# The highest cosine column of a Fourier stage: four partial products in four 32-column strips of TensorE, summed by one more product

## The chip, the cores and the metric

The kernel runs on one core of a Trainium2 chip. Five engines run their own instruction lists in order: PE (TensorE, matrix products into PSUM), DVE (VectorE), ACT (ScalarE), POOL (GpSimd) and SP (SyncE), which here issues most DMAs. An engine waits for another by semaphores. The metric is the device time of one execution in microseconds; a time "before" is the median of three runs.

## The reference

A layer of a diffusion transformer on 2048 positions by 1024 channels: a projection into thirteen pieces, then three branches (short convolution, Fourier mixing, neighbourhood attention), gates, an output projection and a final norm. The change lies in the Fourier branch:

```
def fourier_mix(u):
    b, l, w = u.shape
    ug = u.reshape(b, l, N_FGROUPS, w // N_FGROUPS).astype(jnp.float32)
    y = jnp.fft.fft2(ug, axes=(1, 3), norm='ortho').real
    return y.reshape(b, l, w).astype(u.dtype)
```

Four groups of 128 channels are transformed along 2048 positions and along the 128 channels, and the real part is kept. Only 65 of 128 cosine columns along the channels differ. Columns 0 to 63 of all groups are handled in blocks; column 64 (the highest cosine) of the four groups makes four rows of 2048, and this small product is what the change touches.

## The kernel before

The big projection is made of "pairs": each computes two 128-row output tiles for two blocks by seven products `B11, B21, T2, T1, T3, B22, T4` of 12 matmuls each (lines 315 to 317, 128x512, operands split into a high and a low part; tile `mm`, three PSUM banks). DVE, ACT and POOL prepare the weights (`wh` on ACT, line 131; `wl` on DVE or POOL, line 132) and empty the results (lines 346 to 358 and 428 on DVE).

In the second half of the program a generator, `both()`, yields small steps of attention, then of `fourier()`, between these pair steps. What the generator issues is ordered against the pair's work by a scheduler that writes one fixed list per engine; each engine then keeps to its list.

`fourier()` does for each group g of four:

- SP loads the input `fu` (1 MB, line 1023) into a buffer that it shares with `fold` of the group before, so that the load waits for the last product that reads that `fold`;
- DVE makes even and odd parts `ueo` (lines 1027 and 1030) and folds them to four tiles `fold` (lines 1034 to 1037), POOL fixes single columns (1028, 1031, 1038);
- PE multiplies each fold by the channel table (`s`, line 1044, c = 0 to 3, one PSUM bank for all), and DVE copies the result out to `X` and column 64 to `X64` (1045, 1047) before the next product may write the bank; one more product gives the middle row, copied to `xrow` and `xrow64` (1050 to 1052).

Then the transform along positions. For column 64 (line 1061 on) two halves `par` each take four products of `X64` (128 positions x 4 groups, a stationary operand of 4 columns) with a table tile `tab` of 128x512 (256 KB, six buffers, line 1057), added up in one bank (line 1065), plus the product of the middle row for `par` 0 (1067), and DVE writes the rows out to `y64` (1074, 1075). The blocks of columns 0 to 63 follow with products at lines 1086 and 1094, which take 32 more table tiles; their results `Ym` and `Yr` are stored by SP (1112, 1114). At line 541, early in the program, `mod()` already uses the form that the change brings: products with 32 stationary columns that write four strips of 32 partitions of one bank.

Of the kernel before, what the change touches and what calls it, by code (L numbers as in the profile page):

```python
# [11 lines left out]
F32 = mybir.dt.float32  # L12
F32R = mybir.dt.float32r
AF = mybir.ActivationFunctionType
ALU = mybir.AluOpType
AX = mybir.AxisListType
# [43 lines left out]
def emit(tc, I, out, dbg=None):  # L60
    nc = tc.nc
    dbg = dbg or {}
    stop = dbg.get("stop", "")
    es = ExitStack()

    def pool(stack, name, bufs=1, space=None, side=None):
        kw = {} if space is None else {"space": space}
        if space is not DRAM:
            kw["reuse_waits"] = "tile"
        if side:  # L70
            return Aligned(stack, lambda n_, b_: tc.tile_pool(name=n_, bufs=b_, side=side, **kw), name, bufs)
        return stack.enter_context(tc.tile_pool(name=name, bufs=bufs, **kw))
# [6 lines left out]
    def ctile(name, shape, dt=F32):  # L79
        return cp.tile(shape, dt, tag=name, name=name)  # L80
# [7 lines left out]
    ident = ctile("ident", [128, 128])  # L88
# [58 lines left out]
    def stage():  # L147
        return st.tile([128, 512], F32, tag="st", name="st")
# [856 lines left out]
    def fourier():  # L1005
        ef = ExitStack()
        fp = pool(ef, "fp", 1, None, "right")
        pf = pool(ef, "pf", 1, PSUM)
        X = [fp.tile([128, 4, 4, 64], F32, tag=f"X{c}", name=f"X{c}") for c in range(4)]
        X64 = fp.tile([128, 2, 4, 4], F32, tag="X64", name="X64")  # L1010
        xrow = fp.tile([1, 4, 64], F32, tag="xrow", name="xrow")
        xrow64 = fp.tile([1, 4], F32, tag="xrow64", name="xrow64")
        dct = fp.tile([128, 66], F32, tag="dct", name="dct")
        dst = fp.tile([128, 64], F32, tag="dst", name="dst")
        altr = fp.tile([1, 512], F32, tag="altr", name="altr")
        altc = fp.tile([128, 2], F32, tag="altc", name="altc")
        one2 = fp.tile([1, 2], F32, tag="one2", name="one2")
# [3 lines left out]
        for g in range(4):  # L1021
# [18 lines left out]
            for c in range(4):  # L1040
                w_ = 66 if c < 2 else 64
                ps = pf.tile([128, 4, 128], F32, tag="s1", name="s1")
# [3 lines left out]
                if c < 2:  # L1046
                    nc.vector.tensor_copy(X64[:, c, :, g], ps[:, :, 64])
                yield
            ps = pf.tile([128, 4, 128], F32, tag="s1", name="s1")
# [5 lines left out]
        def table(c, lt):  # L1055
            t = fp.tile([128, 512], F32, tag="tab", name="tab", bufs=6)
            nc.sync.dma_start(t, I["dft"][c, lt])
            return t
# [1 line left out]

        y64 = fp.tile([4, S], F32, tag="big0", name="y64")
        for par in range(2):
            ps = pf.tile([4, 512], F32, tag="x1", name="x1", bufs=2)
            for lt in range(4):
                nc.tensor.matmul(ps, X64[:, par, lt, :], table(par, lt), start=lt == 0, stop=par == 1 and lt == 3)
            if par == 0:
                nc.tensor.matmul(ps, xrow64, altr, start=False, stop=True)
                pe = pf.tile([128, 2], F32, tag="x2", name="x2", bufs=2)
                for lt in range(4):
                    nc.tensor.matmul(pe[:4], X64[:, 0, lt, :], altc, start=lt == 0, stop=False)  # L1070
                nc.tensor.matmul(pe[:4], xrow64, one2, start=False, stop=True)
                nc.vector.tensor_copy(y64[:, 1024:1025], pe[:4, 0:1])
            lo = 1 if par == 0 else 0
            nc.vector.tensor_copy(y64[:, par:1024:2], ps)
            nc.vector.tensor_copy(y64[:, 2048 - par - 2 * lo : 1024 : -2], ps[:, lo:])
            yield
        for g in range(4):
            store(fd[2 + g // 2][(g % 2) * 64 : (g % 2) * 64 + 1, :], y64[g : g + 1, :])
        for t in range(2):
            Ym = fp.tile([128, S], F32, tag="big0", name="Ym")  # L1080
            Yr = fp.tile([128, S], F32, tag="big1", name="Yr")
            for par in range(2):
                gs = slice(2 * t, 2 * t + 2)
                x1 = pf.tile([128, 512], F32, tag="x1", name="x1", bufs=2)
                for lt in range(4):
                    nc.tensor.matmul(x1, X[par][:, lt, gs, :].rearrange("p a b -> p (a b)"), table(par, lt), start=lt == 0,  # L1086
                                     stop=par == 1 and lt == 3)
# [16 lines left out]
                if par == 0:  # L1104
                    pe = pf.tile([128, 2], F32, tag="s1", name="pe")
# [33 lines left out]
    def both():  # L1139
        yield from attention()  # L1140
        vcs.close()
        yield from fourier()
        yield from tail_pools()
# [88 lines left out]
    def branch_bank():  # L1232
        return pc.tile([128, 512], F32, tag="pb", name="pb", bufs=3) if next(turn_) % 2 else bank()

    for b in range(NB):
# [5 lines left out]
        for j in range(8):  # L1241
            acc = None
            for n_, br in enumerate("afc"):
# [3 lines left out]
                ps = branch_bank()  # L1247
# [15 lines left out]
        for t in range(4):  # L1263
# [5 lines left out]
            for x in range(2):  # L1269
# [3 lines left out]
                ps = pc.tile([128, 512], F32, tag="po", name="po")  # L1273
# [106 lines left out]
```

## Time and profile before

| | |
|---|---|
| median of three runs | 2183.29 us (2179.79 to 2183.55) |
| the profiled execution's own time | 2184.33 us |
| its span, first to last instruction | 2182.5 us |
| PE busy | 2111.9 us, 97% of the span |
| DVE, ACT, POOL busy | 64%, 46%, 42% |
| DMA | 336.76 MB, 154 GB/s on average |
| mean granted TensorE clock | 0.987 of full speed |

The profile's times count from the span's start. A row of a timeline gives start, duration, engine, line, operation, output and inputs, shapes and a count; in brackets stands how long the engine had been idle before and what ended that. Matmuls overlap by their pipeline, so the distance between starts, and not the duration, says what one costs. One f32 product is two PE instructions. The Fourier stage lies at about 1520 to 1660 us.

### The profile page before, as it was taken

The page shows a single profiled execution, that of the slowest core. Times are in us where ns is not written, and L with a number is a line of the kernel's source. Part 1 is how long each engine was busy: PE and PEld are TensorE (multiplying, and loading weights), DVE is VectorE, ACT ScalarE, POOL GpSimd, SP SyncE. Part 2 cuts the span into 40 slices and gives each one's busy share as a digit, 9 for nine tenths or more (in the row PEclk, how much of TensorE's full clock was granted, in tenths as well). Part 3 has the DMA queues.
Part 4 walks back from the last instruction along what each step waited for, and adds up shares of the span by engine and source line. Part 5 has one row for each costly group of instructions (what it writes and reads, how often), then busy time and mean ns, then how long its engine had stood idle before and what let it go on. Part 6 is the DMA issues. An engine that isn't in the chain of part 4 may idle for free. (4 is left out here: it accounts for less than half of the span.)

```text
span 2182.5 us, 31772 instructions
## 1 busy us (share of the span) xinstructions
PE 2111.9 (97%) x10612; PEld 1677.0 (77%) x10612; DVE 1394.5 (64%) x2438; ACT 1006.1 (46%) x2191; POOL 907.3 (42%) x701
## 2 busy tenths in 40 slices
PE   7899999999999899999999999999999999999998
PEld 4678888888878687877777777777756778888887
DVE  5774477785765764566677776764735686575752
ACT  3643322334544533466676677776213443233321
POOL 0153477755454654444444344332413241414140
PEclk9899999999999999999999999999999999999999
DMA  8234542346333244344443544543466676666661
GB/s 294 64 120 132 168 145 82 133 168 224 104 102 104 91 142 138 103 129 124 136 145 119 157 144 136 160 148 114 163 206 213 204 242 226 209 221 203 200 196 68
DMA packets 199438, 336.76 MB, mean 154 GB/s; under 512 B 22314, under 2 KB 89194, under 8 KB 198123
## 3 DMA queue, kind: packets, MB, share of 16 engines
q1 hardware_dynamic: 185306, 309.30, 44.5%
q10 hardware_dynamic: 13968, 25.43, 3.1%
q8 instruction: 84, 1.38, 0.3%
q14 instruction: 80, 0.65, 0.1%
HBM read 248.27 MB, written 86.38 MB: 153 GB/s over the span
## 5 line engine op out<-in xcount | busy, mean ns | idle before, releaser
L131 ACT CAST wh<-wr 128x512 fp32r<-128x512 f32 x372 | 229.9, 620 | 458.6 <-PE mm L316 372.1
L132 DVE TENSOR_TENSOR wl<-wr,wh 128x512 fp32r<-128x512 f32 x248 | 238.8, 965 | 43.0 <-ACT wh L131 42.4
L132 POOL TENSOR_TENSOR wl<-wr,wh 128x512 fp32r<-128x512 f32 x124 | 168.0, 1359 | 193.8 <-ACT wh L131 180.0
L342 POOL TENSOR_TENSOR ws<-wr 128x512 f32<-128x512 f32 x62 | 82.3, 1327 | 329.5 <-DMA wr<-w_in 304.2
L373 DVE SCALAR_TENSOR_TENSOR st<-mm,bin,tp 128x512 f32<-128x512 f32 x152 | 113.7, 748 | 141.4 <-PE mm L317 131.9
L132 POOL TENSOR_TENSOR wbl<-wr,wbh 128x512 fp32r<-128x512 f32 x96 | 125.0, 1303 | 159.7 <-ACT wbh L131 151.8
L132 POOL TENSOR_TENSOR wl<-ws,wh 128x512 fp32r<-128x512 f32 x62 | 86.0, 1386 | 124.9 <-ACT wh L131 107.3
L131 ACT CAST wbh<-wr 128x512 fp32r<-128x512 f32 x96 | 59.6, 621 | 146.0 <-DMA wr<-w_br 94.0
L938 PE MATMUL tr<-ident,P 128*128 128x128 f32 (+3 forms) x672 | 119.1, 278 | 4.3 <-ACT PT L948 2.4
L428 DVE TENSOR_TENSOR st<-mm,tp 128x512 f32<-128x512 f32 x96 | 65.9, 686 | 88.5 <-PE mm L317 77.5
L360 POOL TENSOR_TENSOR wr<-wr 128x512 f32<-128x512 f32 x62 | 84.9, 1369 | 83.8 <-DVE wl L132 68.1
L344 POOL TENSOR_TENSOR wr<-ws,wr 128x512 f32<-128x512 f32 x62 | 86.0, 1387 | 77.0 <-DVE wl L132 37.9
L904 ACT ACTIVATE P<-P,sm 128x736 f32<-128x736 f32 (+5 forms) x128 | 104.7, 818 | 25.8 <-DVE sm L903 25.1
L938 PEld LDWEIGHTS tr<-ident,P 128*128 128x128 f32 (+3 forms) x672 | 80.3, 138 | 44.2 <-DVE PT L948 15.7
L317 PE MATMUL mm<-B11h,wl 128*128 128x512 f32 x248 | 99.9, 403 | 9.1 <-DVE wl L132 9.1
L317 PE MATMUL mm<-B22h,wl 128*128 128x512 f32 x260 | 104.1, 400 | 1.9 <-POOL wl L132 1.9
L315 PE MATMUL mm<-B22h,wh 128*128 128x512 f32 x260 | 104.7, 403 | 1.2 <-ACT wh L131 1.2
L316 PE MATMUL mm<-B22l,wh 128*128 128x512 f32 x260 | 103.5, 398 | 0.0
L132 POOL TENSOR_TENSOR KL<-rawk,KH 128x384 fp32r<-128x384 f32 (+1 forms) x64 | 81.4, 1280 | 46.8 <-ACT KH L131 45.3
L315 PE MATMUL mm<-B11h,wh 128*128 128x512 f32 x248 | 100.7, 406 | 0.0
L126 PE MATMUL po<-wo,mh 128*128 128x512 f32 x256 | 99.7, 390 | 0.3 <-DVE u L1170 0.3
L316 PE MATMUL mm<-B11l,wh 128*128 128x512 f32 x248 | 99.9, 403 | 0.0
(370 smaller groups left out, 6343.7 us busy)
## 6 DMA issues: line engine op xcount, KB each, us to landing
wr<-w_in SPq DMA_DIRECT2D x132, 512.0 KB
gd<-st ACTq DMA_DIRECT2D x96, 256.0 KB
wr<-w_br SPq DMA_DIRECT2D x96, 256.0 KB
tg<-gd SPq DMA_DIRECT2D x96, 256.0 KB
tab<-dft SPq DMA_DIRECT2D x40, 256.0 KB
wa<-w_ada SPq DMA_DIRECT2D x32, 256.0 KB
rawq<-qd SPq DMA_DIRECT2D x64, 128.0 KB
rawk<-kd SPq DMA_DIRECT2D x64, 128.0 KB
```

Of the source, the lines that this page charges most:

```text
L126: nc.tensor.matmul(ps, ah, bh, start=first, stop=False)
L131: heng.copy(hi, src) if heng is nc.scalar else heng.tensor_copy(hi, src)
L132: return leng.tensor_tensor(lo, src, hi.bitcast(F32), ALU.subtract)
L315: nc.tensor.matmul(ps, w[0][:, s], oh, start=first and k == 0, stop=False)
L316: nc.tensor.matmul(ps, w[0][:, s], ol, start=False, stop=False)
L317: nc.tensor.matmul(ps, w[1][:, s], oh, start=False, stop=last and k == 3)
L342: ptt(t1, a21, a22, ALU.add)
L344: ptt(a11, t1, a11, ALU.subtract)
L360: ptt(a12, a12, a11, ALU.subtract)
L373: state["ev"] = stt(dst, ps, bc(m), add, ALU.add, ALU.add)
L904: nc.scalar.activation(P[:, : CT + n], P[:, : CT + n], AF.Copy, scale=sm[:, 6:7])
L938: nc.tensor.transpose(pt[:w_, x * 128 : x * 128 + 128], src, ident)
```

## The change

`X64` and `xrow64` get 32 columns per part, of which 28 are zeros set by POOL. The four products of a half write four strips of 32 partitions of one bank instead of adding up in one place. ACT copies that bank to SBUF (`parts`), and one product with a 0/1 matrix `sel4` (made by DVE from the identity) adds the four strips into four rows. One `yield` is added per half.

```
-        X64 = fp.tile([128, 2, 4, 4], F32, tag="X64", name="X64")
+        X64 = fp.tile([128, 2, 4, 32], F32, tag="X64", name="X64")
+        nc.gpsimd.memset(X64, 0.0)
+        sel4 = fp.tile([128, 4], F32, tag="sel4", name="sel4")
+        nc.vector.tensor_reduce(sel4, ident.rearrange("p (c v) -> p v c", v=32)[:, 0:4, :], AX.X, ALU.add)
...
+        xrow64 = fp.tile([1, 32], F32, tag="xrow64", name="xrow64")
+        nc.gpsimd.memset(xrow64, 0.0)
...
-            ps = pf.tile([4, 512], F32, tag="x1", name="x1", bufs=2)
+            four = pf.tile([128, 512], F32, tag="x1", name="x1", bufs=2)
             for lt in range(4):
-                nc.tensor.matmul(ps, X64[:, par, lt, :], table(par, lt), start=lt == 0, stop=par == 1 and lt == 3)
+                nc.tensor.matmul(four[lt * 32 : lt * 32 + 32], X64[:, par, lt, :], table(par, lt), start=True, stop=par == 1 or lt > 0)
             if par == 0:
-                nc.tensor.matmul(ps, xrow64, altr, start=False, stop=True)
+                nc.tensor.matmul(four[0:32], xrow64, altr, start=False, stop=True)
+            parts = stage()
+            nc.scalar.copy(parts, four)
+            yield
+            ps = pf.tile([4, 512], F32, tag="x1", name="x1s", bufs=2)
+            nc.tensor.matmul(ps, sel4, parts, start=True, stop=True)
```

The scheduler writes other lists for the engines. Up to group 1 of the Fourier stage they agree but for the three new small instructions; from group 2 on they differ for some 270 rows of PE's list, and then agree again. Lines of the changed kernel are 4 to 10 higher (1044 is now 1048, 1065 is 1069, 1086 is 1096).

On PE, from the last product of group 2 (`s<-dst,fold`) on, the list before has the rest of the pair's `B21`, and then `T2`, `T1`, `T3` and the start of `B22` ahead of group 3's first product (`s<-dct,fold`); its first rows are:

```order
L1044 MATMUL s_16068<-dst,fold 128x64 x4
L317 MATMUL mm<-B21h_6199,wl_16320 128x512
L315 MATMUL mm<-T2h_6226,wh_16365 128x512
L316 MATMUL mm<-T2l_6227,wh_16365 128x512
L1050 MATMUL s_16074<-dct,ueo 1x66
L317 MATMUL mm<-T2h_6226,wl_16366 128x512
L315 MATMUL mm<-T2h_6231,wh_16365 128x512
L316 MATMUL mm<-T2l_6232,wh_16365 128x512
L317 MATMUL mm<-T2h_6231,wl_16366 128x512
```

In the changed kernel the same place on PE reads, down to the first two products of group 3:

```order
L1048 MATMUL s_16072<-dst,fold 128x64 x4
L315 MATMUL mm<-B21h_6195,wh_16325 128x512
L316 MATMUL mm<-B21l_6196,wh_16325 128x512
L317 MATMUL mm<-B21h_6195,wl_16326 128x512
L1054 MATMUL s_16078<-dct,ueo 1x66
L315 MATMUL mm<-B21h_6199,wh_16325 128x512
L316 MATMUL mm<-B21l_6200,wh_16325 128x512
L317 MATMUL mm<-B21h_6199,wl_16326 128x512
L1048 MATMUL s_16117<-dct,fold 128x66 x4
L1048 MATMUL s_16143<-dct,fold 128x66 x4
```

Group 3's first product stands behind 6 pair matmuls instead of 38 (counted from group 2's last product), and the second directly behind the first, where 8 pair matmuls stood between them. The pair's `T2`, `T1`, `T3` and `B22` now come behind the column-64 products.

On PE, the products of column 64 (`x<-tab,X` and what stands between them) before:

```order
L1044 MATMUL s_16139<-dct,fold 128x66 x4
L1065 MATMUL x_16185<-tab,X_15742 4x512 x2
L1044 MATMUL s_16146<-dst,fold 128x64 x4
L1065 MATMUL x_16185<-tab,X_15742 4x512
L1044 MATMUL s_16152<-dst,fold 128x64 x4
L1065 MATMUL x_16185<-tab,X_15742 4x512
L1050 MATMUL s_16180<-dct,ueo 1x66
L1070 MATMUL x_16199<-altc,X_15742 4x2 x4
L1065 MATMUL x_16230<-tab,X_15742 4x512
L1067 MATMUL x_16185<-altr,xrow_15744 4x512
L1071 MATMUL x_16199<-one_15749,xrow_15744 4x2
L1065 MATMUL x_16230<-tab,X_15742 4x512 x3
```

And on PE in the changed kernel (`x1s` is the sum of the four strips, `st` the copy that ACT makes):

```order
L1069 MATMUL x_16189<-tab,X_15742 32x512
L1048 MATMUL s_16150<-dst,fold 128x64 x4
L1069 MATMUL x_16189<-tab,X_15742 32x512 x3
L1080 MATMUL x_16229<-altc,X_15742 4x2 x4
L1048 MATMUL s_16156<-dst,fold 128x64 x4
L1054 MATMUL s_16184<-dct,ueo 1x66
L1071 MATMUL x_16189<-altr,xrow_15747 32x512
L1081 MATMUL x_16229<-one_15753,xrow_15747 4x2
L1117 MATMUL pe<-altc,X_15738 128x2 x4
L1118 MATMUL pe<-one_15753,xrow 128x2
L1076 MATMUL x1s<-st,sel_15744 4x512
L1069 MATMUL x_16238<-tab,X_15742 32x512 x4
```

The first strip product is apart from its three fellows, the four of the second half stand together, and small products that were later (`pe`) stand between the last addend and the sum.

On DVE, group 3's work before, from the copies of the middle row of group 2 on:

```order
L1052 COPY xrow_15744<-s_16074 1x1
L346 TENSOR_TENSOR tp<-mm,tp 128x512
L132 TENSOR_TENSOR wl_16490<-wr_16292,wh_16489 128x512
L1027 TENSOR_TENSOR ueo<-fu 128x1023
L1030 TENSOR_TENSOR ueo<-fu 128x1023
L350 TENSOR_TENSOR tp<-mm,tp 128x512
L1034 TENSOR_TENSOR fold<-ueo 128x512
L1035 TENSOR_TENSOR fold<-ueo 128x512
L1036 TENSOR_TENSOR fold<-ueo 128x512
L1037 TENSOR_TENSOR fold<-ueo 128x511
L1045 COPY X_15738<-s_16113 128x4x64
```

And on DVE after the change:

```order
L1056 COPY xrow_15747<-s_16078 1x1
L1031 TENSOR_TENSOR ueo<-fu 128x1023
L1034 TENSOR_TENSOR ueo<-fu 128x1023
L1038 TENSOR_TENSOR fold<-ueo 128x512
L1039 TENSOR_TENSOR fold<-ueo 128x512
L1040 TENSOR_TENSOR fold<-ueo 128x512
L1041 TENSOR_TENSOR fold<-ueo 128x511
L1049 COPY X_15738<-s_16117 128x4x64
```

The three instructions for the pair (`tp`, `wl`, `tp`) that stood among group 3's are gone from there.

## Rows read from the trace of the kernel before

**Rows 1.** The page, busy time of each engine.

```profile
PE 2111.9 (97%) x10612; PEld 1677.0 (77%) x10612; DVE 1394.5 (64%) x2438; ACT 1006.1 (46%) x2191; POOL 907.3 (42%) x701
```

**Rows 2.** PE's timeline, 1573 to 1602 us: products of groups 2 and 3.

```profile
1575.90 1.03 PE L1044 MATMUL s<-dst,fold 128*128 128x64 f32 x8
1576.75 0.47 PE L317 MATMUL mm<-B21h,wl 128*128 128x512 f32 x1
...
1586.69 1.08 PE L1044 MATMUL s<-dct,fold 128*128 128x66 f32 x8 [0.63 <-DVE fold L1034]
...
1589.98 1.08 PE L1044 MATMUL s<-dct,fold 128*128 128x66 f32 x8 [0.31 <-DVE X L1047]
```

**Rows 3.** Chain that ended last, 1539 to 1590 us: start, length, what.

```profile
1541.41 4.74 DMA fu<-fud
...
1576.97 5.17 DMA fu<-fud
```

**Rows 4.** DVE's timeline, 1573 to 1590 us.

```profile
1582.23 1.23 DVE L1027 TENSOR_TENSOR ueo<-fu 128x1023 f32<-128x1023 f32 x1 [0.51 <-DMA fu<-fud]
...
1584.51 0.68 DVE L350 TENSOR_TENSOR tp<-mm,tp 128x512 f32<-128x512 f32 x1
1585.11 1.44 DVE L1034 TENSOR_TENSOR fold<-ueo 128x512 f32<-128x512 f32 x1
...
1589.35 0.41 DVE L1045 COPY X<-s 128x256 f32<-128x256 f32 x1
```

**Rows 5.** POOL's timeline, 1573 to 1592 us.

```profile
1587.62 0.09 POOL L1031 MEMSET ueo<- 128x2 f32 x1
```

**Rows 6.** PE's timeline, 1589 to 1602 us: products of column 64.

```profile
1597.94 1.02 PE L1067 MATMUL x<-altr,xrow 1*4 1x512 f32 x2
...
1598.92 2.74 PE L1065 MATMUL x<-tab,X 128*4 128x512 f32 x6
1601.59 0.70 PE L1086 MATMUL x<-tab,X 128*128 128x512 f32 x1
```

**Rows 7.** PE's timeline, 41 to 44 us: the strips of `mod()`.

```profile
41.91 1.07 PE L541 MATMUL pr<-wa,sf 128*32 128x256 f32 x16
42.91 0.50 PE L608 MATMUL mm<-B11h,w1h 128*128 128x512 f32 x1
```

**Rows 8.** ACT, DVE and PE in the timeline, 1589 to 1625 us: copies, small products.

```profile
1596.99 0.21 DVE L1051 COPY xrow<-s 1x64 f32<-1x64 f32 x1 [0.64 <-PE s L1050]
...
1608.95 0.95 PE L1107 MATMUL pe<-altc,X 128*128 128x2 f32 x8
...
1622.88 0.59 ACT L1097 COPY st<-x 128x512 f32<-128x512 f32 x1 [5.66 <-PE x L1094]
```

**Rows 9.** POOL's groups by form: a memset of 128x256.

```profile
L521 POOL MEMSET sf<- 128x256 f32 x1 | 0.3, 311 | 0.0
```

**Rows 10.** PE's timeline, 1636 to 1647 us: a wait and what follows.

```profile
1637.55 0.39 PE L317 MATMUL mm<-T2h,wl 128*128 128x512 f32 x1
1637.77 0.39 PE L315 MATMUL mm<-T2h,wh 128*128 128x512 f32 x1
1640.42 2.69 PE L1086 MATMUL x<-tab,X 128*128 128x512 f32 x4 [2.25 <-DMA tab<-dft]
...
1643.33 0.63 PE L317 MATMUL mm<-T2h,wl 128*128 128x512 f32 x1
1643.76 0.63 PE L315 MATMUL mm<-T2h,wh 128*128 128x512 f32 x1
```

**Rows 11.** Stages: length, each engine's busy time (instructions), granted clock, DMA.

```profile
1640.00:1680.00 40.00, 37.79 (x144) 27.88 (x145) 20.37 (x44) 10.26 (x16) 13.05 (x11) 0.91 0.65 216
```

**Rows 12.** PE's waits, 1560 to 1725 us: total, times, longest.

```profile
PE po L1135 <- DVE dg L1133: 1.8, 1, 1.8
```

**Rows 13.** Chain that ended last, 1560 to 1700 us.

```profile
1627.76 12.62 DMA tab<-dft
...
1659.82 9.43 DMA fd<-Yr
```

More of the change, by code (lines that the diff above doesn't have):

```diff
@@ L1009, in fourier @@
         X = [fp.tile([128, 4, 4, 64], F32, tag=f"X{c}", name=f"X{c}") for c in range(4)]
-        X64 = fp.tile([128, 2, 4, 4], F32, tag="X64", name="X64")
+        X64 = fp.tile([128, 2, 4, 32], F32, tag="X64", name="X64")
+        nc.gpsimd.memset(X64, 0.0)
+        sel4 = fp.tile([128, 4], F32, tag="sel4", name="sel4")
+        nc.vector.tensor_reduce(sel4, ident.rearrange("p (c v) -> p v c", v=32)[:, 0:4, :], AX.X, ALU.add)
         xrow = fp.tile([1, 4, 64], F32, tag="xrow", name="xrow")
-        xrow64 = fp.tile([1, 4], F32, tag="xrow64", name="xrow64")
+        xrow64 = fp.tile([1, 32], F32, tag="xrow64", name="xrow64")
+        nc.gpsimd.memset(xrow64, 0.0)
         dct = fp.tile([128, 66], F32, tag="dct", name="dct")
@@ L1062, in fourier @@
         for par in range(2):
-            ps = pf.tile([4, 512], F32, tag="x1", name="x1", bufs=2)
+            four = pf.tile([128, 512], F32, tag="x1", name="x1", bufs=2)
             for lt in range(4):
-                nc.tensor.matmul(ps, X64[:, par, lt, :], table(par, lt), start=lt == 0, stop=par == 1 and lt == 3)
+                nc.tensor.matmul(four[lt * 32 : lt * 32 + 32], X64[:, par, lt, :], table(par, lt), start=True, stop=par == 1 or lt > 0)
             if par == 0:
-                nc.tensor.matmul(ps, xrow64, altr, start=False, stop=True)
+                nc.tensor.matmul(four[0:32], xrow64, altr, start=False, stop=True)
[4 more added lines that the diff above has]
+            nc.tensor.matmul(ps, sel4, parts, start=True, stop=True)
+            if par == 0:
                 pe = pf.tile([128, 2], F32, tag="x2", name="x2", bufs=2)
                 for lt in range(4):
-                    nc.tensor.matmul(pe[:4], X64[:, 0, lt, :], altc, start=lt == 0, stop=False)
-                nc.tensor.matmul(pe[:4], xrow64, one2, start=False, stop=True)
+                    nc.tensor.matmul(pe[:4], X64[:, 0, lt, :4], altc, start=lt == 0, stop=False)
+                nc.tensor.matmul(pe[:4], xrow64[:, :4], one2, start=False, stop=True)
                 nc.vector.tensor_copy(y64[:, 1024:1025], pe[:4, 0:1])
```

## The prediction

> **What bounds the kernel now.** I read the page first. The reader is to see there that PE is busy for 97% of the span [rows 1], so that an edit counts by what it does to PE's list: the work on it, and the idle time that opens or closes between its entries. Then I read PE's own timeline around the Fourier stage, with PE's waits beside it: between 1560 and 1725 us only four waits carry a name, 2.25 us for a table [rows 10], 1.8 us for DVE's `dg` [rows 12], and under 0.7 us each for a fold or a copy of `X` [rows 2]. Third comes the chain that ended last. It runs here through the load of `fu`, DVE's folds and the `s` products, and not through the pair matmuls [rows 3, 4]. So two strands run side by side: the Fourier chain, which waits most of its time on a DMA and on DVE, and the pair matmuls, which fill PE meanwhile. As long as there is enough filling between two steps of the chain, the chain costs only its own PE work.
>
> The order of the changed kernel shows that this filling is moved. That, and not the saved products, is where I expect most of the effect.
>
> **The change part by part.** All in us of the profiled execution.
>
> *A, the products.* Six PE instructions of the old form take from 1598.92 to 1601.59, 2.67 us [rows 6], so one product (two instructions) costs 0.89, and the eight that go cost 7.1. The new form is shown by `mod()`: eight products of 256 columns in four strips take from 41.91 to 42.91, 1.00 us [rows 7]. Four products of 512 columns are the same number of columns per strip, so a full group costs 1.00. In the new list the first half's group is split: one product alone, 0.89, then three, at most 1.00; the second half's group is whole, 1.00. The two summing products have 4 columns and cost 0.89 each. Added: 4.7, so A = -2.4. The product of the middle row stays, at its old length [rows 6]. If the strips did not overlap at all, the eight would cost 7.1 again and the two sums come on top: A = +1.8. If the split half cost half of what I take, A = -3.3.
>
> The sums need ACT's copy of the bank first, 0.59 for 128x512 with ACT idle in front of it [rows 8]. Between the last addend and the first sum stand the `pe` products, 0.95 [rows 8] and a short one, and before the second sum four pair matmuls of 0.22 each [rows 10]; with some 0.3 of hand-over the copies are covered. I take 0; uncovered, both would add 1.8.
>
> The Trainium skill (TensorEngine Tiling (Array Packing), Performance Considerations, PSUM Bottleneck) speaks against the change here: tiling makes PE faster and leaves the emptying of PSUM as slow as before, so that the copy may become the bound. By that rule the uncovered price holds and the whole sum below would be +10.1 instead of +8.3; no row here shows such a copy right behind strips with PE waiting for it.
>
> *B, the load of group 3.* From the end of group 2's last product (the next start is at 1576.75) to group 3's first product at 1586.69 the chain takes 9.94 [rows 2]: the load, 5.17 [rows 3], then DVE from 1582.23, with one `tp` of the pair between its steps (1584.51 to 1585.11, 0.60) and the first fold, 1.44 [rows 4]. That `tp` is no longer there, so the chain takes 9.3. The load can't start sooner, because its buffer is the fold that the last product reads. Before, 38 pair matmuls at 0.22 to 0.23 stood in that stretch, 8.7 us of filling, and 0.63 was left idle. Now there are 6, 1.4, and the middle row's product: two instructions at 0.11 (eight take 0.85 [rows 2]) and by estimate as much again for the changes of shape around it, 0.35 in all. PE idles 9.3 - 1.75 = 7.6, which is 7.0 more than before. The matmuls that covered it are not lost, they come later and cost there what they cost here. Group 1's load took 4.74 [rows 3]; with that B = +6.6. With the `tp`'s time not saved B = +7.6.
>
> *C, the next product.* Group 3's second product needs the bank that DVE empties with `X` at 1589.35, after all four folds, and the third fold waits for POOL's memset at 1587.62, which stands behind two pair operations of POOL [rows 4, 5]. From the first to the second product it takes 3.29, of which the product is 0.85 (1575.90 to 1576.75 for one like it) [rows 2]. Eight pair matmuls filled the rest but for 0.31. Now nothing stands between: 2.4 idle, C = +2.1. If POOL's two operations are done by then, the folds take 0.6 each and C is +1.0.
>
> *D, the middle row.* Before, old-form products stood around the last `s`, the middle row's product and the addend of that row. Now PE waits there twice for DVE: for a copy of `X`, 0.41 [rows 4], and for the two copies of the row, of which the longer is 0.21 [rows 8], with about 0.2 of hand-over there: 0.6 + 0.5 = 1.1. Below 0.3 it can't go, unless the copies take no time; with double hand-overs it is 1.9.
>
> *E, the clock.* After the wait of 2.25 at 1640.42 the pair matmuls start 0.43 apart (1643.33, 1643.76) instead of 0.22 (1637.55, 1637.77) [rows 10]; that is the 1.2 GHz level. The stage from 1640 to 1680, which holds this wait and the one of 1.8, has a granted clock of 0.91 [rows 11]: 0.09 x 40 = 3.6 us lost, 1.8 per wait. B and C bring two long waits close together. I estimate 2.0 for both, with bounds 0 (the slow time falls into the idle time) and 4 (1.8 for each and a little more).
>
> *F, the later stage.* The 32 table products come between pair matmuls in a new rhythm. The two waits of before and the slow clock behind them are worth 2.25 + 1.8 + 3.6 = 7.7 in all. The table's wait stems from a load that landed 12.62 after its issue, behind the stores of `Ym` and `Yr` [rows 13]; these stand in SP's list before the last nine tables as they stood before the last eight, so I let it stay. The wait for `dg` hangs on the store of `Yr`, 9.43 [rows 13], and PE asks for it 12 matmuls later than before; I let half of it and of its slow clock go: F = -1.5. Bounds: -7.7, all gone, and +4, one more such wait.
>
> *Small ones.* The memset of 128x256 on POOL is 0.3 [rows 9], the reduction for `sel4` at most as long as a copy of `X`, 0.41 [rows 4]. Both come a group or more before they are used, and both engines idle there: 0, at most 0.3 if POOL's `wl` behind it is asked for at that moment, and no gain. The zeros in 28 of 32 columns cost PE nothing beyond A.
>
> Sum: -2.4 + 7.0 + 2.1 + 1.1 + 2.0 - 1.5 = +8.3. On the profiled execution's 2184.33 that gives 2192.6. The median of the three runs is 1.04 lower, and the same step from 2183.29 gives 2191.6, which is the forecast.
>
> **The rivals.**
>
> *The Fourier chain, and not PE's list, sets the end of the stage (not slower).* The chain of waits speaks for it, since from 1560 us on it follows the chain [rows 3, 13]. The chain itself gets shorter: 0.6 of the `tp`, and 2.4 of products. If the later stage has room for the displaced matmuls, 40 x 0.22 = 9 us, then the end comes 3.0 earlier: 2180.3. Against it: the room that the trace shows there is 7.7 (F), clock included, and it would have to go to the last bit. It decides from the point where F reaches -9.8, which cancels A to E, and for the full 3.0 it must reach -12.8; with F at its bound of -7.7 the sum is +2.1, 2185.4, within what I call the same.
>
> *The clock stays low through the clump (slower still).* Group 3's products and the strips are short and stand between waits, so PE is not filled until the pair's `T2`. If all of that, four `s` products at 0.85, the strips, sums and the middle row, some 8 us, ran at 1.2 GHz, E would be 8 and the sum +14.3: 2197.6. For it: the two waits in a row. Against it: the one wait of 2.25 in the trace was followed by no more than a few slow matmuls [rows 10].
>
> *The strips don't overlap at 512 columns (the change doesn't do what it says).* Then A = +1.8 and the sum is +12.5: 2195.8. Against it stand the strips of `mod()` [rows 7].
>
> **How the numbers follow.** A measurement of this kernel can tell 0.2% from no change, 4.4 us: faster is below 2178.9, slower above 2187.7. The forecast with its own range (2187 to 2195, A to E moved by their smaller bounds, F between -4 and 0) gets 0.62. The chain as the bound, from 2178 to 2186, gets 0.18, of which 0.06 is faster. The low clock gets 0.15, and strips without overlap 0.05. Slower: all of the low clock and the strips, 0.20, and 0.54 of the forecast's 0.62 after some mass for its lower edge: 0.74. Same: 0.12 of the chain and 0.08 of the forecast, 0.20. The range must reach into the chain's upper half and to the low clock's time: 2183.5 to 2198.
>
> **What would show it right or wrong.** Right: PE's timeline has one idle stretch of 7 to 8 us before group 3's first `dct` product, ended by DVE's fold, and a second of 2 to 2.5 before the next one, ended by the copy of `X`; matmul starts 0.43 apart behind them; four strip instructions per 0.45 us in the second half's group; and the pair's `T2` to `B22` at full pace later, with the wait for the table still there. B is wrong if the idle stretch is under 5; A if the second half's group takes 3 us or more; F if PE has no wait of over 1 us between the tables and the `dg` products. The whole is wrong, and the chain is the bound, if these idle stretches are there and the kernel is still not slower.

## The result, and the profile after

The changed kernel takes 2199.3 us (median of four runs, 2194.5 to 2202.1) against 2182.8 for the kernel before: ratio 1.0079, 95% interval 1.0063 to 1.0095. A second set of runs (e5 below) gave 1.0071, 1.0052 to 1.0090. So it is slower by some 16 us, as the forecast said in sign, and twice as far as the forecast's +8.3. It lies 1.3 us above the range. The profiled execution took 2194.5, the shortest of the four.

The page of the changed kernel hardly shows it. TensorE's share is one point lower than in [rows 1], with four more instructions:

```profile
PE 2110.9 (96%) x10616; PEld 1676.3 (76%) x10616; DVE 1392.1 (63%) x2439; ACT 1008.0 (46%) x2193; POOL 906.1 (41%) x703
```

PE's timeline from group 2's last pair matmul to the pair's `T2` does show it (start, length, line, out<-in, in brackets the idle time before it and what ended it). It answers to [rows 2, 6]:

```profile
1575.30 0.40 PE L317 MATMUL mm<-B21h,wl 128*128 128x512 f32 x1
1583.41 1.95 PE L1048 MATMUL s<-dct,fold 128*128 128x66 f32 x8 [7.71 <-DVE fold L1038]
1586.69 1.94 PE L1048 MATMUL s<-dct,fold 128*128 128x66 f32 x8 [1.34 <-DVE X L1051]
1588.56 1.91 PE L1069 MATMUL x<-tab,X 128*32 128x512 f32 x2
1590.40 1.97 PE L1048 MATMUL s<-dst,fold 128*128 128x64 f32 x8
1592.30 1.07 PE L1069 MATMUL x<-tab,X 128*32 128x512 f32 x3
...
1593.16 1.07 PE L1069 MATMUL x<-tab,X 128*32 128x512 f32 x3
...
1596.65 0.38 PE L1054 MATMUL s<-dct,ueo 128*1 128x66 f32 x2 [0.52 <-DVE X L1049]
1597.40 1.91 PE L1071 MATMUL x<-altr,xrow 1*32 1x512 f32 x2 [0.37 <-DVE xrow L1056]
...
1605.08 0.51 PE L315 MATMUL mm<-T2h,wh 128*128 128x512 f32 x1
1605.42 0.40 PE L316 MATMUL mm<-T2l,wh 128*128 128x512 f32 x1
1605.66 0.40 PE L317 MATMUL mm<-T2h,wl 128*128 128x512 f32 x1
```

Two things are to be read here. The first is the idle time: 7.71 before group 3's first product, 1.34 before its second, 0.52 and 0.37 at the middle row. The second is the length of everything behind the first wait. A group's `s` product has 1.95 where [rows 2] has 1.08 for the same eight instructions, and the addend of the middle row 1.91 where [rows 6] has 1.02. The stages say why (length, busy time and instructions of PE, PEld, DVE, ACT, POOL, granted clock, DMA share, GB/s):

```profile
1583.40:1605.10 21.70, 19.47 (x75) 10.92 (x75) 7.13 (x16) 1.21 (x2) 1.58 (x3) 0.50 0.20 61
1605.10:1640.00 34.90, 34.90 (x111) 20.15 (x111) 13.59 (x24) 8.16 (x13) 3.86 (x3) 1.00 0.65 223
1640.00:1690.00 50.00, 48.16 (x195) 34.33 (x193) 20.31 (x42) 13.74 (x22) 15.66 (x13) 1.00 0.66 220
```

For 21.7 us after the wait TensorE is at its 1.2 GHz level, though it is busy for 19.5 of them. The upper level is back at the first pair matmuls, whose starts stand 0.34, then 0.24 apart. Later the clock is at 1.00, where [rows 11] had 0.91. The wait for a table and the one for `dg` are shorter than in [rows 10, 12] (PE's waits, 1560 to 1740 us: total, times, longest):

```profile
PE x L1104 <- DMA tab<-dft: 1.2, 1, 1.2
PE po L1145 <- DVE dg L1143: 0.9, 2, 0.6
```

The chain from the load of `fu` is on DVE's timeline, and answers to [rows 4]; DVE waits 3.98 for the load, and the folds follow without a `tp` between:

```profile
1579.09 1.22 DVE L1031 TENSOR_TENSOR ueo<-fu 128x1023 f32<-128x1023 f32 x1 [3.98 <-DMA fu<-fud]
1580.23 1.22 DVE L1034 TENSOR_TENSOR ueo<-fu 128x1023 f32<-128x1023 f32 x1
1581.56 1.71 DVE L1038 TENSOR_TENSOR fold<-ueo 128x512 f32<-128x512 f32 x1
1583.18 1.75 DVE L1039 TENSOR_TENSOR fold<-ueo 128x512 f32<-128x512 f32 x1
1584.86 0.68 DVE L1040 TENSOR_TENSOR fold<-ueo 128x512 f32<-128x512 f32 x1
1585.46 0.68 DVE L1041 TENSOR_TENSOR fold<-ueo 128x511 f32<-128x511 f32 x1
1586.06 0.41 DVE L1049 COPY X<-s 128x256 f32<-128x256 f32 x1
1586.40 0.15 DVE L1051 COPY X<-s 128x4 f32<-128x4 f32 x1
```

To compare whole executions I use two marks on PE: the first Fourier product and the tail's first product. In the kernel before they stand here:

```profile
1532.60 1.11 PE L1044 MATMUL s<-dct,fold 128*128 128x66 f32 x8
1670.55 0.68 PE L1135 MATMUL po<-dg,ones 128*128 128x128 f32 x4
```

and in the changed one here:

```profile
1530.06 1.11 PE L1048 MATMUL s<-dct,fold 128*128 128x66 f32 x8
1684.35 0.68 PE L1145 MATMUL po<-dg,ones 128*128 128x128 f32 x4
```

That is 137.95 against 154.29, +16.3 between the marks. Of this, 12 pair matmuls (2.7 us at 0.227) have only moved from behind the second mark to before it, so that +13.6 is left. Up to the first mark, where nothing is changed, the executions already differ by 2.5 us, so one profile against one profile (+10.2) understates the change.

### The profile page after: what moved, and what is told of

Its sections match the earlier page's. It is cut to its first block, busy times and chain, and to the rows that moved or that the text cites. A ratio compares the mean times of both kernels' runs of the same rounds, so it can differ in the third digit from the quotient of the medians.

```text
span 2192.7 us, 31780 instructions
## 1 busy us (share of the span) xinstructions
PE 2110.9 (96%) x10616; PEld 1676.3 (76%) x10616; DVE 1392.1 (63%) x2439; ACT 1008.0 (46%) x2193; POOL 906.1 (41%) x703
## 5 line engine op out<-in xcount | busy, mean ns | idle before, releaser
L315 PE MATMUL mm<-T4h,wh 128*128 128x512 f32 x248 | 99.4, 401 | 0.4 <-ACT yh L131 0.4
```

The costliest lines, as they stand in the source:

```text
L315: nc.tensor.matmul(ps, w[0][:, s], oh, start=first and k == 0, stop=False)
```

## The experiments

The two theories that I set against each other: the *order theory*, by which the time comes from group 3 standing early in PE's list (waits, and a low clock behind them), and the *strips theory*, by which the strips, their copy and the summing product cost it. The order theory comes with a supposed cause: `parts = stage()` takes one of the pair's four staging buffers in rotation, so that later results of the pair would have to wait for the column-64 work, and the scheduler would bring that work, with group 3, forward.

**e1, another buffer for the copy.**

```diff
-            parts = stage()
+            parts = fp.tile([128, S], F32, tag="big1", name="parts")[:, :512]
```

> The changed kernel, with the strips' copy in ueo's buffer (free there) in place of a staging tile; the instructions' order around group 3 is then again that of before (36 products of the pair between group 2's middle row and group 3's first dct product, where the changed kernel has 6). Order theory (the 10 to 16 us come from group 3 standing early, and that from the staging tile, which lies ahead of the pair's own staging tiles in the rotation): no idle of 7 us ahead of group 3, no long stretch at 1.2 GHz, and only the products' gain is left: 2 to 4 us faster than before, 2178.5 to 2182 us (ratio 0.998 to 1.000). Strips theory (the strips, their copy and the summing product cost the time themselves, since they stand in the Fourier chain): still 8 us or more slower than before, ratio 1.004 or more.

Measured: 2180.4, ratio 0.9989 (0.9976 to 1.0001). That one line takes away the whole loss; whether it gains anything this interval, which holds 1, does not say (e8 does). In PE's list 38 pair matmuls stand again between group 2's last `dst` product and group 3's first `dct` product, where the changed kernel has 6. PE's timeline of e1, around the strips:

```profile
1585.99 1.08 PE L1048 MATMUL s<-dct,fold 128*128 128x66 f32 x8 [1.96 <-DVE fold L1038]
...
1591.34 1.07 PE L1069 MATMUL x<-tab,X 128*32 128x512 f32 x8
1592.22 0.34 PE L1080 MATMUL x<-altc,X 128*4 128x2 f32 x8
...
1603.39 1.02 PE L1076 MATMUL x1s<-parts,sel 128*4 128x512 f32 x2 [0.42 <-ACT parts L1073]
```

(The expectation's 36, counted from the middle row, are 35 in the trace; its 6 are counted from the last `dst` product.) The idle time is 1.96 instead of 7.71, and those 2 us need not be the edit's: the kernel before waits 1.97 at this place in its second profile (e9). The four strips of a half (eight instructions) take 0.88 from start to the next start, which is what one of the old products took [rows 6]. The strips theory falls. The second sum does wait 0.42 for ScalarE's copy.

**e2, the old products, and only a staging copy added.**

```diff
+            parts = stage()
+            nc.scalar.copy(parts[:4], ps)
+            yield
-            nc.vector.tensor_copy(y64[:, par:1024:2], ps)
+            nc.vector.tensor_copy(y64[:, par:1024:2], parts[:4])
...
```

(the second copy to `y64` reads `parts` likewise)

> The kernel before with its eight 4-column products, and only this added: each half's result is copied by ScalarE into a staging tile before VectorE spreads it. That alone moves group 3 to the same early place as in the changed kernel. Order theory: DVE's fold ends an idle of 7 to 8 us before group 3's first dct product, the clock is granted at 0.50 for about 20 us behind it, and the kernel is 10 to 18 us slower than before (2193 to 2201 us, ratio 1.005 to 1.008), as the changed kernel is. Strips theory: the old products are there, so within 3 us of before.

Measured: 2195.96, ratio 1.0055 (1.0035 to 1.0075). Without a single strip, the loss is there. PE's waits in e2, 1560 to 1740 us:

```profile
PE s L1044 <- DVE fold L1034: 6.3, 1, 6.3
PE s L1044 <- DVE X L1047: 3.4, 2, 2.6
```

and its granted clock (seventh value after the times) in four stages behind them, with two rows of PE's timeline:

```profile
1585.00:1595.00 10.00, 9.11 (x28) 5.48 (x28) 1.67 (x6) 0.00 (x0) 0.00 (x0) 0.50 0.14 42
1595.00:1605.00 10.00, 10.00 (x25) 1.62 (x25) 2.79 (x8) 1.20 (x2) 0.00 (x0) 0.50 0.34 114
...
1606.00:1607.00 1.00, 1.00 (x3) 0.13 (x1) 0.00 (x0) 0.00 (x0) 0.00 (x0) 0.66 0.59 209
1607.00:1608.00 1.00, 1.00 (x4) 0.39 (x3) 0.00 (x0) 0.52 (x2) 0.00 (x0) 1.00 0.62 193
```

```profile
1601.07 6.37 PE L1065 MATMUL x<-tab,X 128*4 128x512 f32 x8
...
1614.33 0.79 PE L315 MATMUL mm<-T2h,wh 128*128 128x512 f32 x1
```

The first wait is 6.3, a little under the 7 to 8 expected. The upper level comes back between 1606 and 1607, in the last of the old 4-column products, and so before the first pair matmul at 1614.33. Together e1 and e2 show that the staging tile is what moves group 3: e1 keeps the copy and the `yield` and changes the tile alone, and in e2 the tile, with a copy and a `yield`, moves group 3 in the kernel before too. Whether strips are worth anything at this early place stays open: the intervals of e2 and of the changed kernel overlap.

**e3, the wait filled.**

```diff
+            if g == 3:
+                dm = pf.tile([128, 512], F32, tag="x2", name="fill", bufs=2)
+                oh = state["op"]["B11", 0][0]
+                for n_ in range(32):
+                    i = nc.tensor.matmul(dm, oh[:, :128], oh, start=n_ == 0, stop=n_ == 31)
...
```

(the lines left out tie them behind group 2's middle row and ahead of group 3's first product; like the pair's matmuls, and unlike the f32 products of the Fourier stage, each is one PE instruction)

> The changed kernel with 32 useless 128x512 products (7.4 us at 0.23 each) put on TensorE between group 2's middle row and group 3's first dct product, where it stands idle 7.7 us; nothing reads them. Idle-brings-the-clock-down theory: the clump of short products then runs at 2.4 GHz, the time is 8 to 10 us less than the changed kernel's, 2187 to 2192 us (ratio 1.002 to 1.004), and the pair's products behind it are as late as the waits alone make them. Clump theory (the short products between waits of 0.4 to 1.3 us are themselves what keeps the clock at 1.2 GHz): the stretch from group 3's first product on stays at 0.50 or falls to it within some us, and the time is within 3 us of the changed kernel's.

Measured: 2188.83, ratio 1.0029 (1.0017 to 1.0041), 9 to 11 us less than the changed kernel by the ratios (0.42 and 0.50%), with 7.5 us more of work on PE. PE's timeline of e3:

```profile
1572.28 7.55 PE L1048 MATMUL fill<-B11h 128*128 128x512 f32 x32
...
1580.15 1.08 PE L1056 MATMUL s<-dct,fold 128*128 128x66 f32 x8
...
1582.36 1.08 PE L1056 MATMUL s<-dct,fold 128*128 128x66 f32 x8 [0.61 <-DVE X L1061]
...
1591.39 2.19 PE L1079 MATMUL x<-tab,X 128*32 128x512 f32 x5
1593.52 0.79 PE L315 MATMUL mm<-T2h,wh 128*128 128x512 f32 x1
```

and the stage that answers to 1583.40 to 1605.10 of the changed kernel:

```profile
1580.10:1593.50 13.40, 11.85 (x76) 6.52 (x76) 6.00 (x16) 1.82 (x3) 3.79 (x3) 0.94 0.40 137
```

The clump (group 3's products and the column-64 products behind them) now has its full-clock lengths (1.08), and slows only at its end. PE is busy in it for 11.85, of which two of the pair's matmuls that moved in here are 0.5: 11.4, where the changed kernel has 19.47 for the same work. That is 8.1 us for the clock, and 9.7 (half of 19.47) if the end of the clump had kept the upper level too. The idle-brings-the-clock-down theory holds, and the clump theory, by which the clump is slow with or without the long wait, falls. But the clock does drop once here without a long wait before it: it is 1.00 up to 1591 and 0.50 from 1592 to 1595, at the clump's end and in the first pair matmuls.

**e4, group 3 later, staging tile kept.** Eleven empty background steps ahead of group 3:

```diff
+            if g == 3:
+                for _ in range(11):
+                    yield
```

> The changed kernel, staging tile and all, with eleven empty background steps ahead of group 3, so that its load and products are issued some four products of the pair later: group 3's first dct product again stands behind 36 products of the pair, as before. Order theory: as e1, 1 to 4 us faster than before if the eleven steps cost nothing at the end (2179 to 2182 us); where they push the last of the background work behind the last pair, up to 5 us more. Staging theory (the tile that the pair's results have to wait for costs the time, wherever group 3 stands): 8 us or more slower than before, with waits of ScalarE or VectorE for a staging tile in the pair.

Measured: 2178.57, ratio 0.9985 (0.9971 to 0.9999). The staging tile is still taken, and it costs nothing once group 3's products stand behind the pair's. So the loss is the place in the list and not the waiting for a buffer. PE's longest wait for the fold in e4 is 0.7 us, and the clock is 1.00 from 1560 to 1690:

```profile
1583.43 1.08 PE L1051 MATMUL s<-dct,fold 128*128 128x66 f32 x8 [0.66 <-DVE fold L1041]
```

**e5, the changed kernel again.** No edit.

> The changed kernel again, unaltered, beside more runs of before on one chip. Its one profiled execution was 10.2 us over the profiled one of before, but the medians stood 16.5 us apart. Theory that the terms are those of the early group 3 alone (products -2.4, waits +8.7, clock +9 to +11, nothing later): ratio 1.0065 to 1.0085, 2196 to 2201 us, a wait of 7 to 8 us for the fold and some 20 us at 0.50 again. Theory that a gain of 6 us in the last stage belongs to the change (the waits for a table, for the tail's operands and the clock at 0.91 that the profile of before has there): ratio 1.0045 or less, 2192 us.

Measured: 2196.91, ratio 1.0071 (1.0052 to 1.0090). The smaller effect of 1.0045 is outside the interval. The marks in its profile:

```profile
1531.23 1.11 PE L1048 MATMUL s<-dct,fold 128*128 128x66 f32 x8
1686.02 0.68 PE L1145 MATMUL po<-dg,ones 128*128 128x128 f32 x4
```

154.79 between them, within 0.5 of the first profile; its wait for the fold is 7.68, and the clump 21.68.

**e6, both cures.** The buffer of e1 and the steps of e4.

> The changed kernel with both cures: the strips' copy in ueo's buffer (e1) and eleven empty background steps ahead of group 3 (e4). Order theory: group 3's load then lands before its products are due, so the wait for the fold (2.0 us in e1, 0.7 in e4) is at most 0.7 and no stretch falls to the lower clock around it; 2 to 6 us faster than before, 2176 to 2180 us (ratio 0.9973 to 0.999). If the eleven steps push Fourier's last work behind the last pair, within 0.1% of before instead.

Measured: 2184.19, ratio 1.0010 (0.9997 to 1.0024): a miss, and no better than before. PE's waits in e6, 1560 to 1740 us:

```profile
PE s L1051 <- DVE fold L1041: 2.6, 2, 1.9
PE mm L315 <- DVE tp L358: 2.2, 1, 2.2
PE pe L1120 <- DVE Yr L1123: 1.4, 1, 1.4
```

The expectation read the waits of 2.0 (e1) and 0.7 (e4) as the two kernels' own, but this wait changes from execution to execution: 0.63 and 1.97 in the two profiles of before, 1.96 and 0.23 in those of e1's kernel (e1, e8). The time is the one named for Fourier's last work being pushed behind the last pair, but that did not happen: the last table products start at 1660.80, and pair matmuls follow until after 1700. A wait for `Yr` stands there that e1 and e4 don't have, and the clock is 0.91 from 1590 to 1610 and 0.94 from 1610 to 1640, where e4 has 1.00. Why e6 has these, and so the 5.5 us against e4, stays open.

**e7, the old products, with the wait filled as in e3.** The fill alone, added to the kernel before, brings group 3 forward there too: beside the 32, four pair matmuls stand ahead of its first product instead of 38, though the eight between its first and its second stay.

> The kernel before with its old products, and 32 useless 128x512 products (7.4 us) put between group 2's middle row and group 3's first dct product; that moves group 3 early as well, so the idle there is filled. TensorE-bound theory: work or waiting at this place costs its length, and with no idle the clock stays up: 6 to 9 us slower than before (2188.5 to 2191.5 us, ratio 1.003 to 1.004), so 4 to 8 us less than e2, which has the same products early and unfilled. Fourier-chain theory (VectorE's and the DMA's chain sets the end, TensorE has room): within 3 us of before. Clump theory (the clump of short products takes the clock down by itself): as e2, 1.0055.

Measured: 2188.57, ratio 1.0030 (1.0017 to 1.0044). Useless work of 7.5 us at this place costs 6.5 (3.7 to 9.6 by the interval): TensorE's list sets the end of the stage, so the rival "the Fourier chain, and not PE's list, sets the end" falls. The old products point to the clock's part too: filled, the granted clock is 1.00 from 1590 to 1610, where e2 has 0.50, and by the ratios they are 5.5 us faster than unfilled (e2), though the two intervals overlap.

**e8, e1 again, and e9, the kernel before against itself.**

> The kernel of e1 again (strips, their copy in ueo's buffer, the order of before), to say whether the strips alone gain anything: its first interval, 0.9976 to 1.0001, still holds no change. If four strips in the time of one of the old products are worth the 2.4 us that the prediction gave them: ratio 0.998 to 0.9995 again, with 0.88 us for the four strips of a half. If the first result was chance: 0.9995 to 1.001.

> The kernel before, unaltered, against itself, for what a comparison here says when nothing is changed and for a second profiled execution. Theory that the clock of 0.91 and the waits of 2.3 and 1.8 us in the last stage belong to the one execution that was profiled: from the first Fourier product to the tail's first product some 3 to 5 us less than the 138.0 us of the first profile. Theory that they belong to the kernel: 137 to 139 us again. Ratio 0.9985 to 1.0015 by either.

Measured: e8 2178.9, ratio 0.9983 (0.9974 to 0.9993); e9 2180.93, ratio 0.9999 (0.9989 to 1.0009). With e1, the edit in the old order gains 2.4 and 3.7 us by the two ratios; the second is clear of no change. The four strips of the first half take 0.88 in e8 as well (1589.77 to 1590.65). The marks of e9:

```profile
1528.17 1.11 PE L1044 MATMUL s<-dct,fold 128*128 128x66 f32 x8
1665.13 0.68 PE L1135 MATMUL po<-dg,ones 128*128 128x128 f32 x4
```

136.96, where the first profile had 137.95 (so e5 against e9, less the 12 moved matmuls, is +15.1 between the marks): the theory that 3 to 5 us of the last stage belong to one execution falls. The wait for `dg` is 1.8 again in e9, the one for a table 1.4 instead of 2.3.

## Why the prediction came out too low

Its working by its own letters, against what was measured:

- **A, products, -2.4: held.** The strips overlap; four take 0.88 (e1). In the old order the edit gains 2.4 (e1) and 3.7 us (e8), of which 0.9 is a shorter wait for `dg` in both. The rival "strips don't overlap" falls. In the changed kernel the second half's group and the first sum take 3.5 together (1601.58 to 1605.08), at half the clock, so the prediction's sign against A (3 us or more) would have misled. The Trainium skill (TensorEngine Tiling (Array Packing), Performance Considerations, PSUM Bottleneck) says that the copy may become the bound: where it stands close behind the strips PE waits 0.42 for it (e1), and none in the changed kernel.
- **B, load of group 3, +7.0: held.** Idle 7.71, where 0.63 was before: +7.1. Two small errors cancel in it: the chain took 9.75 and not 9.3, and the filling lasted 2.0 and not 1.75. Against the 1.97 of e9 it is +5.7.
- **C, second product, +2.1: +1.0 came** (1.34 - 0.31), the figure of the lower bound, but by luck and not for its reason. From the first product to the second it takes 3.28 (1583.41 to 1586.69), as long as before (3.29), so the folds were no quicker; at the lower clock the first product itself takes 1.95 of that, and less is left to wait. Nor did the memset hold the third fold in [rows 4, 5]: before as after (1588.14, 1584.86) that fold follows the second without a pause. It is the second fold that is slow in both, 1.75, while POOL's operation L343 runs; in e3, where none of the pair's POOL operations falls there, it takes 0.69 and the two products start 2.21 apart.
- **D, middle row, +1.1:** 0.52 + 0.37 = 0.9. (The forecast's second part, 0.5, adds up to 0.4 from its own 0.21 and 0.2.)
- **E, the clock: this is the step that failed.** The prediction put it as "I estimate 2.0 for both, with bounds 0 [...] and 4". It measured 8.1 against e3, whose own clump slows at its end, and up to 9.7: at least twice the upper bound. I took the price from [rows 10, 11]: after a wait of 2.25 PE was slow for a few pair matmuls, 1.8 us lost per wait. What I carried over was the price of a wait, and what it costs is the work done until the clock is back. In [rows 10] a few pair matmuls and table products were done by then, here the whole column-64 clump, 19.47 us of it. What kept the clock low so long is not shown: the waits here are longer and more (7.71, 1.34, 0.52, 0.37 against 2.25), and other work stands behind them. That it needs the pair's matmuls to come back is refuted by e2, where it came back in 4-column products. A short wait has no fixed price either: behind 1.96 in e1 the pair matmuls start 0.43 apart for a while, behind 1.97 in e9 the clock stays at 1.00. The rival "the clock stays low through the clump" said what happened, with the right size (E = 8, 2197.6), and I gave it 0.15; its reason, short products between waits, is not enough by itself, since with the long wait filled (e3) the same clump ran at the upper level for 11 us. My argument against it was a row that had no clump behind its wait, and so could not speak on it.
- **F, later stage, -1.5: too small.** The wait for `dg` fell by 0.9 (1.8 in e9 too) and the one for a table by 1.0 in the profiled pair, but the latter was 1.4 in e9 as well. The clock of 1640 to 1680 is 0.91 in before, 0.96 in e9 and 1.00 in the changed kernel, which is 3.6 and 1.6 us. Together that is -5.5 against the first profile and -2.7 against e9. The claim that the table's wait stays held (1.2), though it was shorter. (Half of the `dg` wait and of its slow clock, as the forecast priced them, would be -1.8 and not -1.5.)

With E at 8.1 to 9.7, and B, C and D as measured, the forecast's sum is -2.4 + 7.1 + 1.0 + 0.9 + E - 1.5 = +13.2 to +14.8, which is 2196.5 to 2198.1 from the median that the forecast started from. With F as measured it is +9.2 to +13.6. The two comparisons say +16.5 and +15.8, with intervals that begin at +13.8 and +11.3; what is left over, 1 to 7 us, is not assigned. Between the marks of the first two profiles the account closes: of the +13.6, 6.6 are A to D, -1.0 is the table's wait and -1.7 the low clock behind it in before (0.57 from 1641 to 1645), which leaves 9.7 for E, half of 19.47.

The Trainium skill (TensorE: Matmul & The Clock Gate, HAM oscillation — how this bites in real kernels) describes bursts of work that begin at the lower clock after each wait for a DMA, and advises an arrangement of the loop that keeps PE at the upper one. The trace agrees: 19.47 us of work behind the wait, which here is for DVE's fold behind a load, and 11.4 with the wait filled (e3); with the pair's matmuls back in front of group 3 (e4) the clock is 1.00 throughout.

What the prediction did not see at all is why group 3 had moved. It took the new order as given by the products. The order came from one line, the staging tile (e1, e2), and without it the change is a small gain. That it acts through the rotation of the four buffers is how I read it; the runs show that the tile moves the order, not by which step.

## What to carry to other kernels

A temporary from a buffer that others use too can change an order far from its own place: when a scheduler works out the lists, look at which pool a new tile comes from before blaming or crediting the arithmetic. Price a long idle stretch of TensorE by the idle time plus what the work behind it may cost at the lower clock (here 7.7 and up to 9.7 us). A price read off one short wait need not hold for a longer one with other work behind it.

## What the runs showed that I had not expected

The low clock lasted 21.7 us with PE busy for 19.5 of them (0.50 throughout), and in e2 for 20 us and more. In the changed kernel it rose as the pair's 128x512 matmuls came back, in e2 within the old 4-column products. In e3 the same clump began at the upper level and kept it for most of its length before it slowed. And useless matmuls paid for themselves: filling the wait for 7.5 us made the changed kernel 9 to 11 us faster. Between two executions of the same kernel, the time up to the first Fourier product alone differs by 4.4 us (1532.60 in before, 1528.17 in e9), so differences of a few us need the marks, not the spans.
